# One layer of a gMLP and convolution decoder on eight cores: the mixer in one pass, the convolution on column tiles, normalisations beside the matmuls

## Chip, cores, metric

The kernel runs on all 8 cores of one Trainium2 chip, each on its own tokens with the same weights. The metric is the time of the slowest core in microseconds (us). Most executions agree within 0.3%. Some fall in a slower state, in which the cores of one die, sometimes of both, are granted a lower Tensor engine clock; those are kept out of every comparison here. PE is the Tensor engine, PEld its weight loads, DVE the Vector engine, ACT the Scalar engine, POOL GpSimd and SP the Sync engine.

## The reference, cut

```python
# D_MODEL = D_A = D_B = 2048, D_FF = 5632, CHUNK = 128, K_CONV = 31
x = x + 0.5 * swiglu_ffn(rms_norm(x, ffn1_norm), ffn1_w_gu, ffn1_w_down)
h = rms_norm(x, mix_norm)
ua, va, glu_a, glu_b, gate_a, gate_b = split(h @ w_in)          # 6 x 2048
v   = layer_norm(gelu(va))
y_a = chunk_spatial_gating(gelu(ua), v, w_s, b_s) @ w_pa
g   = glu_a * sigmoid(glu_b)
c   = silu(layer_norm(depthwise_conv31(concat(conv_prev, g)) + b_dw))
y_b = c @ w_pb
x   = x + (sigmoid(gate_a) * y_a + sigmoid(gate_b) * y_b) @ w_out
x = x + 0.5 * swiglu_ffn(rms_norm(x, ffn2_norm), ffn2_w_gu, ffn2_w_down)
return rms_norm(x, final_norm), ...                             # and v and g states
```

Each core holds 1024 prompt tokens, 64 sample tokens (16 sequences of 4) and 30 to 32 tokens of history, which the convolution needs from the half before.

## The kernel before

Activations lie with channels on the partitions and tokens in the columns. Weights are float32 in memory and are cast to bfloat16 by the DMA that loads them. x is transposed on PE at the start, y at the end. The mixer runs twice, over 608 and then 512 columns, with a barrier of all engines between its stages. A normalisation stands in the foreground (this cut and the next are shortened):

```python
def rms(gidx, segs, Hout):
    for (x0, n, l0) in segs:
        for k in range(KC):                      # sq: a ring of two buffers
            ea = act(sq, X[:, k, x0:x0 + n], AF.Square)
            mm(bk, ONES, sq, k == 0, k == KC - 1, deps=[ea])
        # Sqrt on ACT, reciprocal on DVE, then 16 scalings on DVE
...
mixer_pass(0, True)        # segs (0, 512) and 96 columns of history and samples
mixer_pass(512, False)
```

The convolution multiplies by 31 diagonal 128x128 matrices for each block of 128 channels:

```python
edg = tt(DG, IDF.to_broadcast([128, 31, 128]), wdw.to_broadcast([128, 31, 128]), ALU.mult)
for k in range(31):
    mm(bc[:, 0:512], DG[:, k, :], GPB[:, k:k + 512], k == 0, k == 30)
```

Of the kernel before, what the change touches and what calls it, by code (L numbers as in the profile page):

```python
# [5 lines left out]
F32 = mybir.dt.float32  # L6
# [7 lines left out]
NT = 1120  # L14
NPV = 9 * 16 + 31 * 16
PV_F1, PV_MIX, PV_F2, PV_FIN, PV_BDW, PV_LCG, PV_LCB, PV_LVG, PV_LVB = range(9)
PV_WDW = 9 * 16
EPS = 1e-6
ENGS = ["pe", "act", "dve", "pool", "sp"]
NSLOT = 4  # L20
SLOT_B = 8192

OFF_X = 0
OFF_PV = 71680
OFF_IDF = OFF_PV + 2560
OFF_ONES = OFF_IDF + 512
OFF_EPS = OFF_ONES + 256
OFF_GTAIL = OFF_EPS + 16
OFF_WST = OFF_GTAIL + 1920
OFF_MS = OFF_WST + 4096  # L30
OFF_SMALL = OFF_MS + 2048
PL0 = 83456
assert OFF_SMALL + 256 <= PL0
OFF_RSTD = PL0
OFF_SLOTS = OFF_RSTD + 4608
OFF_TMPX = OFF_SLOTS + NSLOT * SLOT_B
REG0 = OFF_TMPX + 12288
OFF_H = REG0
OFF_HID = REG0 + 35840
OFF_HM = REG0  # L40
OFF_V = REG0 + 19456
OFF_US = OFF_V + 20480
OFF_CN = OFF_US + 18432
ARENA_B = REG0 + 78848

class Plan:
    def __init__(self):
        self.q = {e: [] for e in ENGS}
        self.n = {e: 0 for e in ENGS}
        self.waited = {e: {} for e in ENGS}  # L50
        self.dcnt = {}
        self.needed = {e: set() for e in ENGS}

    def wait(self, eng, ev):
        if ev is None:
            return
        k, v = ev
        if self.waited[eng].get(k, 0) >= v:
            return
        self.waited[eng][k] = v  # L60
        if k in self.needed:
            self.needed[k].add(v)
        self.q[eng].append(("wait", k, v))

    def op(self, eng, fn, deps=()):
        for d in deps:
            self.wait(eng, d)
        self.n[eng] += 1
        self.q[eng].append(("op", fn, self.n[eng]))
        return (eng, self.n[eng])  # L70

    def dma(self, eng, out, in_, semkey, deps=()):
        for d in deps:
            self.wait(eng, d)
        c = self.dcnt.get(semkey, 0) + 16
        self.dcnt[semkey] = c
        self.q[eng].append(("dma", out, in_, semkey))
        return (semkey, c)

    def last(self, eng):  # L80
        return (eng, self.n[eng]) if self.n[eng] > 0 else None

class Ring:
    def __init__(self, items):
        self.items = items
        self.i = 0
        self.free = [[] for _ in items]

    def get(self):
        idx = self.i % len(self.items)  # L90
        self.i += 1
        return idx, self.items[idx], list(self.free[idx])

    def release(self, idx, events):
        self.free[idx] = [e for e in events if e is not None]

def build_program(stop_after=None):
# [7 lines left out]

    xin = din("xin", [NT, D])
    cache = din("cache", [16, 30, D])
    pv_d = din("pv", [128, NPV])
    identf_d = din("identf", [128, 128])
# [7 lines left out]
    w_gu1 = din("w_gu1", [44, 128, 4096])  # L117
    w_dn1 = din("w_dn1", [32, 128, 2816])
    w_v = din("w_v", [8, 128, 4096])
    w_u = din("w_u", [8, 128, 4096])  # L120
    w_glu = din("w_glu", [16, 128, 4096])
    w_gate = din("w_gate", [16, 128, 4096])
    w_pab = din("w_pab", [16, 128, 4096])
    w_out = din("w_out", [8, 128, 4096])
    w_gu2 = din("w_gu2", [44, 128, 4096])
    w_dn2 = din("w_dn2", [32, 128, 2816])

    y_o = dout("y", [1088, D])
    vlast_o = dout("vlast", [128, D])
    vsamp_o = dout("vsamp", [64, D])  # L130
    csp_o = dout("csp", [30, D])
    cssn_o = dout("cssn", [64, D])
    csso_o = dout("csso", [16, 26, D])

    P = Plan()

    with nc.sbuf_tensor("arena", [128, ARENA_B // 4], F32) as arena, \
            nc.psum_tensor("ps", [128, 8, 512], F32) as ps:

        def view(off, shape, dt=F32):  # L140
            esz = 4 if dt == F32 else 2
            n = int(np.prod(shape))
            a = arena[:, off // 4:(off + n * esz) // 4]
            if dt != F32:
                a = a.bitcast(dt)
            if len(shape) == 2:
                a = a.rearrange("p (a b) -> p a b", a=shape[0])
            elif len(shape) == 3:
                a = a.rearrange("p (a b c) -> p a b c", a=shape[0], b=shape[1])
            return a  # L150

        X = view(OFF_X, [KC, NT])
        PV = view(OFF_PV, [NPV])
        IDF = view(OFF_IDF, [128])
        ONES = view(OFF_ONES, [128], BF16)
        EPSV = view(OFF_EPS, [4])
        GTAIL = view(OFF_GTAIL, [KC, 30])
        WST = view(OFF_WST, [16, 128], BF16)
        MS = view(OFF_MS, [16, 64], BF16)
        SMALL = view(OFF_SMALL, [64])  # L160
        ST = SMALL[:, 0:24]
        MV = SMALL[:, 24:26]
        RS1 = SMALL[:, 28:29]
        RSTD = view(OFF_RSTD, [1152])
        slots = [view(OFF_SLOTS + i * SLOT_B, [4096], BF16) for i in range(NSLOT)]
        H = view(OFF_H, [KC, NT], BF16)
        HID = view(OFF_HID, [11, NT], BF16)
        HM = view(OFF_HM, [KC, 608], BF16)
        V = view(OFF_V, [5, D], BF16)
        MM_ = view(OFF_V, [KC, 576], BF16)  # L170
        US = view(OFF_US, [KC, 576], BF16)
        CN = view(OFF_CN, [KC, 576], BF16)

        banks = Ring([ps[:, b, :] for b in range(8)])
        wring = Ring(slots)

        def mm(out, lhsT, rhs, start, stop, deps=()):
            return P.op("pe", lambda e: e.matmul(out, lhsT, rhs, start=start, stop=stop), deps)  # L178

        def tr(out, in_, ident, deps=()):  # L180
            return P.op("pe", lambda e: e.transpose(out, in_, ident), deps)  # L181

        def act(out, in_, func, deps=(), **kw):
            return P.op("act", lambda e: e.activation(out=out, in_=in_, func=func, **kw), deps)  # L184

        def cp(eng, out, in_, deps=()):
            if eng == "act":
                return P.op("act", lambda e: e.copy(out=out, in_=in_), deps)  # L188
            return P.op(eng, lambda e: e.tensor_copy(out=out, in_=in_), deps)  # L189

        def tt(out, in0, in1, op, deps=(), eng="dve"):
            return P.op(eng, lambda e: e.tensor_tensor(out=out, in0=in0, in1=in1, op=op), deps)  # L192

        def ts(out, in0, s1, s2, op0, op1, deps=(), eng="dve"):
            return P.op(eng, lambda e: e.tensor_scalar(out=out, in0=in0, scalar1=s1, scalar2=s2,
                                                       op0=op0, op1=op1), deps)

        def stt(out, in0, scalar, in1, op0, op1, deps=(), eng="dve"):
            return P.op(eng, lambda e: e.scalar_tensor_tensor(out=out, in0=in0, scalar=scalar, in1=in1,  # L199
                                                              op0=op0, op1=op1), deps)  # L200

        def barrier():
            evs = [P.last(e) for e in ("pe", "act", "dve", "pool")]
            evs = [e for e in evs if e is not None]
            for ok_ in sorted(k for k in P.dcnt if k.startswith("o_")):
                evs.append((ok_, P.dcnt[ok_]))
            for e in ("pe", "act", "dve"):
                for ev in evs:
                    if ev[0] != e:
                        P.wait(e, ev)  # L210
            return evs

        w_hold = []

        def wload(parts, extra=()):
            idx, slot, free = wring.get()
            ev = None
            extra = list(extra) + list(w_hold)
            del w_hold[:]
            for i, (dst_fn, src) in enumerate(parts):  # L220
                ev = P.dma("pool", dst_fn(slot), src, "w%d" % idx, deps=(free + list(extra)) if i == 0 else ())
            return idx, slot, ev

        def wk(slot, n):
            return slot[:, 0:16 * n].rearrange("p (k n) -> p k n", n=n)

        def colblk(w, c0, n):
            return w[:, c0:c0 + n].rearrange("(k p) n -> p k n", p=128)

        MT = view(OFF_H, [128])  # L230
        MSK = view(OFF_H + 512, [64])
        WCOL = view(OFF_H + 1024, [16, 4])
        WSTT = view(OFF_H + 2048, [16, 128])
        c_ev = None
        for dst, src in ((PV, pv_d), (IDF, identf_d), (MT, maskt_d), (MSK[0:64], masks_d),
                         (WCOL[0:64], wcol_d), (WSTT, wst_d)):
            c_ev = P.dma("sp", dst, src, "c0")
        P.op("dve", lambda e: e.memset(ONES, 1.0))
# [10 lines left out]
        for t in range(9):  # L249
# [3 lines left out]
            if t == 6:  # L253
                w_hold.append(lev)
# [450 lines left out]
        if stop_after != "p0":  # L705
            ffn(PV_F1, w_gu1, w_dn1)
# [204 lines left out]
```

## Time and profile before

| | before |
|---|---|
| median of the runs before the prediction | 3789.4 us (4 runs) |
| profiled run, slowest core | 3786.8 us |
| PE busy, share of the span | 3507.9 us, 93% |
| mean granted clock | 0.957 |
| DMA moved | 328 MB |

A busy PE is not a PE at its peak: matmuls are pipelined, so their rate has to be read from pieces of the chain of waits and not from the mean of one instruction. The prediction below shows these pieces, the windows by stage and the waits.

### The profile page before, as it was taken

How to read it: one execution, taken by the hardware profiler on the slowest of the kernel's cores; microseconds unless marked ns; L12 is line 12 of the kernel's file. 1: busy time of each engine (PE TensorE's matmuls, PEld its weight loads, DVE VectorE, ACT ScalarE, POOL GpSimd, SP SyncE). 2: the span in 40 equal slices, each digit the busy share in tenths (PEclk: the TensorE clock that was granted, in tenths of full speed). 3: DMA queues.
4: the chain of work that ended last, by engine and by line, in shares of the span. 5: the costliest groups of instructions: out<-in, count | busy, mean ns of one | idle time of the engine just before them, and what ended most of it. 6: DMA issues, size and time to landing. Idle time of an engine off the chain costs nothing.

```text
span 3786.8 us, 53265 instructions; the slowest of 8 cores (3777.8 to 3786.8 us)
## 1 busy us (share of the span) xinstructions
PE 3507.9 (93%) x22280; PEld 2021.7 (53%) x22280; DVE 937.4 (25%) x1517; ACT 501.2 (13%) x970; POOL 170.1 (4%) x316
## 2 busy tenths in 40 slices
PE   5999999999976999879977998799899999999996
PEld 3666666666645555435545443344466666666663
DVE  5112121121132433331122433211412112112125
ACT  3000000000012111221112112200300000000003
POOL 0000000000000000000000000000000000000000
PEclk7999999999988999989988999899899999999997
DMA  8334334343335443247656643588333434334332
GB/s 194 67 58 83 64 65 78 58 83 67 58 82 102 91 96 82 53 82 136 132 119 126 119 79 57 101 152 146 69 64 65 78 57 83 67 58 83 64 54 95
DMA packets 50537, 328.44 MB, mean 87 GB/s; under 512 B 6208, under 2 KB 7968, under 8 KB 17248
## 3 DMA queue, kind: packets, MB, share of 16 engines
q0 software_dynamic: 43904, 293.36, 42.7%
q1 hardware_dynamic: 6400, 31.67, 2.7%
q8 instruction: 182, 2.98, 0.3%
q14 instruction: 51, 0.42, 0.0%
HBM read 603.16 MB, written 14.66 MB: 163 GB/s over the span
## 4 chain that ended last, share of the span: by engine, by line
PE 90%; DVE 4%; ACT 2%; DMA 2%; issue 1%; DVEq 0%; SPq 0%; ACTq 0%; POOLq 0%
PE ps L178 90%; DVE arena L199 2%; ACT arena L184 2%; DVE arena L192 1%; DMA arena<-xin 1%; PE ps L181 1%; DVE arena L382 0%; DMA y<-arena 0%; ACT L184 0%; DVE arena L286 0%; DVE arena L633 0%; DVE arena L727 0%; DMA arena<-cache 0%; DMA vsamp<-arena 0%; DMA vlast<-arena 0%
## 5 line engine op out<-in xcount | busy, mean ns | idle before, releaser
L178 PE MATMUL ps<-arena 128*128 128x374 bf16 (+5 forms) x21896 | 3459.2, 319 | 221.8 <-ACT arena L184 117.2
L178 PEld LDWEIGHTS ps<-arena 128*128 128x128 bf16 x21896 | 1973.8, 98 | 1703.3 <-issue 319.4
L192 DVE TENSOR_TENSOR arena<-arena,ps 128x374 bf16<-128x374 f32 (+6 forms) x424 | 221.3, 527 | 1709.0 <-PE ps L178 1175.1
L184 ACT ACTIVATE arena<-ps 128x374 f32<-128x374 f32 (+5 forms) x528 | 246.5, 467 | 2508.0 <-PE ps L178 2504.7
L199 DVE SCALAR_TENSOR_TENSOR arena<-ps,arena 128x374 f32<-128x374 f32 (+3 forms) x451 | 244.2, 547 | 528.8 <-PE ps L178 528.0
L192 DVE TENSOR_TENSOR arena<-arena 128x512 bf16<-128x512 f32 (+5 forms) x198 | 245.2, 1251 | 194.7 <-PE ps L181 161.2
L184 ACT ACTIVATE arena<-arena 128x512 bf16<-128x512 f32 (+9 forms) x277 | 159.8, 613 | 353.0 <-DVE arena L199 180.1
L199 DVE SCALAR_TENSOR_TENSOR arena<-arena 128x374 bf16<-128x374 f32 (+7 forms) x204 | 103.1, 578 | 2.6
L181 PE MATMUL ps<-arena 128*128 128x128 f32 (+4 forms) x384 | 58.5, 306 | 48.7 <-DMA arena<-xin 28.4
L787 POOL DMA_DIRECT2D arena<-w_gu x88 | 46.7, 531 | 1202.9 <-PE ps L178 1156.3
L181 PEld LDWEIGHTS ps<-arena 128*128 128x128 f32 (+4 forms) x384 | 49.4, 157 | 53.0 <-issue 51.0
L787 POOL DMA_DIRECT2D arena<-w_dn x64 | 33.8, 529 | 794.9 <-PE ps L178 794.9
L184 ACT ACTIVATE arena<-ps,arena 128x512 bf16<-128x512 f32 (+6 forms) x60 | 37.5, 624 | 213.2 <-PE ps L178 213.1
L382 DVE BATCH_NORM_STATS2 arena<-arena 128x6 f32<-128x512 bf16 (+1 forms) x36 | 22.2, 679 | 121.8 <-ACT arena L184 121.6
L192 DVE TENSOR_TENSOR arena<-ps,arena 128x512 f32<-128x512 f32 (+1 forms) x64 | 27.7, 454 | 97.3 <-PE ps L178 97.3
L184 ACT ACT_TABLE_LOAD x20 | 25.7, 1283 | 132.8 <-PE ps L178 99.6
L787 POOL DMA_DIRECT2D arena<-w_pab x32 | 16.9, 529 | 457.4 <-PE ps L178 457.4
L188 ACT COPY arena<-ps 128x512 f32<-128x512 f32 (+4 forms) x68 | 30.8, 464 | 47.6 <-PE ps L181 35.7
L286 DVE RECIPROCAL arena<-arena 128x374 f32<-128x374 f32 (+3 forms) x9 | 22.3, 2482 | 50.9 <-ACT arena L184 50.9
L189 DVE COPY arena<-ps 128x512 f32<-128x512 f32 (+2 forms) x36 | 23.7, 680 | 34.4 <-PE ps L181 24.4
L787 POOL DMA_DIRECT2D arena<-w_glu x32 | 17.3, 542 | 182.7 <-PE ps L178 182.7
L787 POOL DMA_DIRECT2D arena<-w_gate x32 | 16.9, 529 | 144.1 <-PE ps L178 138.4
(19 smaller groups left out, 83.0 us busy)
## 6 DMA issues: line engine op xcount, KB each, us to landing
arena<-w_gu POOLq DMA_DIRECT2D x88, 1024.0 KB, 8.0
arena<-w_dn POOLq DMA_DIRECT2D x64, 704.0 KB, 6.3
arena<-w_glu POOLq DMA_DIRECT2D x32, 1024.0 KB, 8.1
arena<-w_pab POOLq DMA_DIRECT2D x32, 1024.0 KB, 8.6
arena<-w_gate POOLq DMA_DIRECT2D x32, 1024.0 KB, 9.3
arena<-w_v POOLq DMA_DIRECT2D x16, 1024.0 KB, 8.8
arena<-w_u POOLq DMA_DIRECT2D x16, 1024.0 KB, 8.6
arena<-w_out POOLq DMA_DIRECT2D x16, 1024.0 KB, 9.0
```

Source lines behind the costliest of these rows:

```text
L178: return P.op("pe", lambda e: e.matmul(out, lhsT, rhs, start=start, stop=stop), deps)
L181: return P.op("pe", lambda e: e.transpose(out, in_, ident), deps)
L184: return P.op("act", lambda e: e.activation(out=out, in_=in_, func=func, **kw), deps)
L188: return P.op("act", lambda e: e.copy(out=out, in_=in_), deps)
L189: return P.op(eng, lambda e: e.tensor_copy(out=out, in_=in_), deps)
L192: return P.op(eng, lambda e: e.tensor_tensor(out=out, in0=in0, in1=in1, op=op), deps)
L199: return P.op(eng, lambda e: e.scalar_tensor_tensor(out=out, in0=in0, scalar=scalar, in1=in1, op0=op0, op1=op1), deps)
L286: er = P.op("dve", lambda e, l0=l0, n=n: e.reciprocal(out=RSTD[:, l0:l0 + n], in_=RSTD[:, l0:l0 + n]), deps=[ea])
L382: e0 = P.op("dve", lambda e, q=q, t=t, rows=rows, STp=STp: e.bn_stats(out=STp[0:rows, q * 6:(q + 1) * 6], in_=V[0:rows, t, q * 512:(q + 1) ...
L787: ins = e.dma_start(out=item[1], in_=item[2])
```

## The change

The intent was to take away PE columns and PE idle time together. The host hands over x and takes y channel by channel, so that the transposes go. The mixer runs once over all columns. The convolution keeps four shifted copies of its input on four groups of 32 partitions, so that one matmul covers four taps of 32 channels. Four such matmuls, with their outputs on four groups of 32 columns of the array (column tiles), cover four taps of a block of 128 channels, and eight such quads cover its 31 taps. The normalisations that follow an FFN or the output projection begin beside its last pass. Barriers are replaced by dependencies tracked by memory cell. To make room, x is spilled to memory during the mixer. The core of the diff, with comments added:

```diff
-NT = 1120
+NP_ = 1024
+NS = 64
+NH = 30
+NM = NP_ + NS
+NT = NM + NH
-NSLOT = 4
+NSLOT = 5
...
-            for k in range(31):
-                lc = mm(bc[:, 0:512], DG[:, k, :], GPB[:, k:k + 512], k == 0, k == 30, ...)
+            P.dma("sp", gs_d[c % 2], g, wk=[("gs", c % 2)])             # spill g
+            for s in range(4):                                          # read it back shifted by s
+                P.dma("sp", g4[32 * s:32 * s + 32, :, 0:GPN], src[:, :, s:s + GPN], ...)
...
+            for (c0, n) in ((0, 512), (512, 512), (1024, 64)):
+                bk = bank()
+                for q in range(8):
+                    for j in range(4):
+                        mm(bk[32 * j:32 * j + 32, 0:n], dg[:, q, j, :], rhs, q == 0, q == 7)
...
-        mixer_pass(0, True)
-        mixer_pass(512, False)
...
+        P1 = [[(0, 384), (384, 384)], [(768, NT - 768)]]    # last down pass of FFN1, in two
+        def after_m1(pi, o, m, seg):
+            add_square(X1, m, o == 0, *seg)
+            if pi == 1:
+                if o == 0:
+                    stats1(0)
+                    stats1(1)
+                bgpop(1 if o < 3 else 2)                     # scalings of the norm, one or two at a time
```

## The prediction

> **What bounds the kernel now.** I read the page's busy shares first, then the matmuls by shape, then one table of windows cut at the stage borders (found in the chain of waits in order of time), then the waits of the Tensor engine. The Tensor engine (PE) is busy 93% of 3786.8 us; no other engine passes 25%. By shape:
>
> ```profile
> L178 PE MATMUL ps<-arena 128*128 128x374 bf16 x8512 | 1404.8, 323 | 24.0 <-ACT arena L184 16.5 <-DVE arena L192 7.2
> L178 PE MATMUL ps<-arena 128*128 128x512 bf16 x5224 | 1182.1, 383 | 150.5 <-ACT arena L184 84.7 <-DMA vsamp<-arena 29.0 <-DMA vlast<-arena 24.8
> L178 PE MATMUL ps<-arena 128*128 128x64 bf16 x1824 | 71.3, 196 | 3.5 <-ACT arena L184 3.5
> ```
>
> The means (323 ns for 374 columns) are latencies of pipelined instructions; the rate is in the chain. A piece of 1584 matmuls is one FFN quarter (1056 gate/up, 528 down):
>
> ```profile
> 252.71 250.81 PE ps L178 x1584
> 504.41 250.81 PE ps L178 x1584
> 1585.49 1.22 PE ps L178 x8
> ```
>
> From 252.71 to 504.41 are 251.70 us for 1584 matmuls of 373.3 columns on average: 158.9 ns each, that is 373.3/2.4 = 155.6 ns plus 3.3 ns. So inside a stage nothing but columns counts. The windows show where that is not so (columns: busy us and count of PE, PEld, DVE, ACT, POOL, then clock, DMA share, GB/s):
>
> ```profile
> 0.00:95.00 95.00, 54.40 (x258) 31.85 (x259) 48.62 (x75) 37.35 (x73) 2.46 (x8) 0.78 0.86 193
> 95.00:1099.00 1004.00, 997.29 (x6281) 610.01 (x6279) 176.22 (x324) 68.63 (x140) 40.17 (x76) 1.00 0.38 70
> 1099.00:1128.00 29.00, 10.09 (x38) 4.36 (x38) 18.46 (x34) 9.44 (x25) 0.00 (x0) 0.50 0.23 73
> 1199.00:1306.00 107.00, 76.26 (x596) 42.26 (x596) 51.69 (x115) 28.29 (x45) 3.17 (x6) 0.86 0.37 75
> 1306.00:1583.00 277.00, 270.02 (x2096) 148.79 (x2096) 89.37 (x96) 42.90 (x97) 23.32 (x35) 0.98 0.45 89
> 1583.00:1631.00 48.00, 9.96 (x65) 4.15 (x66) 29.44 (x39) 27.48 (x37) 0.00 (x0) 0.64 0.00 1
> 2388.00:2675.00 287.00, 281.94 (x1286) 126.52 (x1286) 44.14 (x64) 23.21 (x40) 21.14 (x40) 0.99 0.84 144
> 3716.00:3786.80 70.80, 40.08 (x190) 24.19 (x189) 43.08 (x69) 32.98 (x67) 0.00 (x0) 0.67 0.34 127
> ```
>
> Long windows run at PE 97 to 99% and clock 0.98 to 1.00; the seams (start, normalisations, end) run nearly empty and at a clock down to 0.50. So the mean clock, 0.957, comes from idle seams and not from density. The waits name what stands in the seams:
>
> ```profile
> PE ps L178 <- ACT arena L184: 117.2, 94, 36.3
> PE ps L178 <- DVE arena L199: 31.4, 4, 16.5
> PE ps L178 <- DMA vsamp<-arena: 29.0, 1, 29.0
> PE ps L181 <- DMA arena<-xin: 28.4, 7, 15.2
> PE ps L178 <- DMA vlast<-arena: 24.8, 1, 24.8
> ```
>
> **What the Trainium skill says.** (1) "TensorE: Matmul & The Clock Gate", section "Back-to-back issue gap", gives N/2.4 + 2.5 ns for a warm matmul; the trace agrees within 1 ns (158.9 against 158.1), for weights loaded behind the stream. (2) The same page, "Seeing it yourself", says all-core dense matmul should be budgeted at 13/16 of the clock. The trace disagrees: 1.00 over a thousand microseconds on eight cores. I therefore do not expect a denser kernel to be throttled. (3) The same page, "Measured speedup vs the span model", has three column tiles of 32 outputs running 2.38 times as fast as one after another; "TensorEngine Tiling", "Restrictions", adds that column tiling gives up the fast weight load. No run here shows it; the kernel before has no such matmul. (4) "VectorE: DVE Perf Modes", "The perf-mode tier table", gives 693 ns for a 2048-element bf16 tensor_scalar in SBUF. No instruction before shows it (its f32 two-input pass of that width took 2.29 us).
>
> **The change part by part.** It is a rewrite: dependencies are tracked by memory cells rather than barriers, the mixer runs once over all columns instead of in two token halves, x and y come transposed from the host, and the convolution is remapped.
>
> Dense parts before, from the chain: FFNs 2 x 6336 x 158.9 ns = 2014 us; v projection 132; u and spatial gating 137; GLU and convolution 487 (16 periods of 16.73 in the first half, 13.71 in the second); merge and output projection 599. Sum 3370; the other 417 us are seams.
>
> Dense parts after, at N/2.4 + 3.3 ns:
> - FFN1: 1118 columns instead of 1120: 2112 x (1118/2.4 + 10) = 1005 us. FFN2 drops the history columns and runs 1088: 1936 x 463.4 ns + 176 x 465 ns = 979. Together 1984, saving 30.
> - v projection: 576 matmuls of 512 columns instead of 1152 of 256, at 217 ns (63 convolution matmuls of the second half take 13.7 us): 125, saving 7.
> - GLU: 512 x (1118/2.4 + 10) = 244, saving 2. u: 256 x 463.4 = 119, plus 144 small spatial matmuls at about 60 = 9; 127, saving 10. Merge and output: 1280 x 463.4 = 593, saving 6; the sliver matmuls of 64 and 96 columns, which cost about 50 ns (63 of them in 16.73 - 13.6 = 3.1 us), are gone there.
> - Convolution: before, 31 diagonal 128x128 matmuls per channel block, 512 columns twice and 64 once: 16 x (31 x 2 x 217.8 + 31 x 50 ns) = 241 us. After, the history is stored four times with shifts on four partition groups, so one matmul handles 4 taps of 32 channels and writes 32 outputs; 8 tap groups x 4 channel groups, the four being column tiles that may run together. Full overlap would be 8 x 1088/2.4 x 16 = 58 us. I allow 240 ns for a quad of 512 columns (256 quads, 61 us) and 110 for one of 64 (128, 14 us), an estimate between full overlap and the skill's 79% efficiency (2.38 of 3): 75, saving 166.
>
> Sum after 3148, saving 222.
>
> Seams. Start, about 90 us before the first steady FFN matmul: the 256 f32 transposes of x and their evictions go, what remains is the load: 9.2 MB at an estimated 200 to 300 GB/s (the hardware queue before moved 31.67 MB in 2.7% of the span of 16 engines, 310 GB/s, with larger packets), three weight tiles squeezed in, then one sum of squares. All three segments' sums stand before the first gate matmul in PE order, so I put it at 50 us. End, 71 us: y is stored untransposed and two thirds of the final norm run during the last down passes. But the last pass, 128 columns, takes PE only 10 us while Vector scales a 512 segment in it (3.35 reciprocal + 16 x 0.74) and adds 32 small ops of about 0.25: 23 us. So 12 us of backlog, then the last segment's chain (table load 1.28, reciprocal 0.9, 16 x 0.34, a store of 3): 25 us in all. Inside: the two entry norms, two v layernorms, two conv layernorms and the FFN2 norm, some 250 us, become background work. I leave 45: 5 at FFN1 to v, 6 where the v layernorm (about 23 us of Vector) outlasts the 20 us that eight banks let PE run ahead, 12 where the conv sums, six f32 matmuls and three root/reciprocal chains precede the u stage, 9 at its end and at FFN2's entry, and 13 for cold clock and Vector's load in the u stage (2.25 us of 2.7 per segment). Seams after: 120.
>
> 3148 + 120 + 2 (launch, as before) = 3270; I add 10 for the unseen and say 3280 us.
>
> **Rivals.** A: the column tiles do not overlap. Then 1024 x 217 + 512 x 40 ns = 242 us instead of 75, and the kernel takes about 3445. For it: no such matmul in the trace; against: the skill's measurement. B: transfers become the bound in the GLU and convolution stage. Each channel block now moves 1.05 MB of weights (FFN window: 70 GB/s at share 0.38, so 5.7 us of all engines), 0.4 MB of spill and 1.6 MB of shifted reads in pieces of 1 to 2 KB (7 to 9 us): some 16 us in a 20 us period. Tight; if the small pieces are twice as dear the stage grows by 50 to 80 us, to 3340. Two blocks of run-ahead speak against latency trouble. C: full density brings throttling, 13/16 on all matmuls: over 3700. The clock of 1.00 in both FFNs speaks against. D: Vector or the new GpSimd multiplies (48 of 364 columns, none in the trace before) become the bound of the u stage: 20 to 40 us. E: the seams close wholly: 3235. That the weight loads of the mixer halve (share 0.84 in the second merge) gains nothing: that window is already at PE 98%.
>
> **Range and chances.** A at about 8%, B at 15%, D at 15% (parts of them overlap), the start and end uncertain by 20 us each way: 3225 to 3370 eight times in ten. Everything except C is more than 2% faster: faster 0.97, same 0.02, slower 0.01.
>
> **What would show it.** Right: FFN pieces still at about 158.9 ns, mean clock 0.98 or more, GLU and convolution at about 20 us per channel block, PE over 96% busy, first FFN matmul near 50 us, tail near 25. Wrong: a convolution block of 15 us instead of 5 (A); PE waiting for the shifted copies with the DMA share near 1 (B); FFN clock under 0.95 (C); PE waiting for Vector in the u stage (D).

## The result

The changed kernel takes 3273.14 us (median of 11 runs, 3270.82 to 3887.81, slow ones included) against 3792.83 (16 runs). The ratio is 0.8631, with a 95% interval of 0.8621 to 0.864. A ratio here is the mean time of one kernel's fast runs over that of the other's in the same rounds, so it is not quite the ratio of the medians. The prediction was 3280, 7 us high.

The first profile of it fell in the slow state, so it was profiled again among the experiments, unedited, under the name e0_after:

> The changed kernel itself, unedited, beside the edited ones on the same chip, and for a profile in the fast state. Expected 3273 us, as in its first runs, mean clock 0.99 on both dies; it is the mark that the other runs are compared with.

On that chip die 0 was granted a little less clock in every run, and the median was 3291.63 (ratio 0.8685, 0.8659 to 0.8711). Die 1 was undisturbed. For this reason I read core 6, on die 1, and compare kernels below also by the median core of an undisturbed die: 3265.4 us for the unedited kernel (the first result's fast runs have 3262.8 to 3267.2 on both dies). The cores of that profile:

```profile
die 0 (median of its cores): 3283.5 us, clock 0.985
die 1 (median of its cores): 3265.6 us, clock 0.991
```

The same windows as in the prediction, cut at the new stage borders (busy us and count of PE, PEld, DVE, ACT, POOL, then clock, DMA share, GB/s). They are the start, FFN1, the entry of v, v, GLU and convolution, the way to u, u, merge and output, FFN2, and the end:

```profile
0.00:50.00 50.00, 17.60 (x43) 4.46 (x43) 22.07 (x37) 21.25 (x47) 2.53 (x9) 1.00 0.89 232
50.00:1056.50 1006.50, 1005.64 (x6346) 614.44 (x6345) 216.52 (x397) 92.38 (x186) 41.25 (x78) 1.00 0.42 70
1056.50:1068.10 11.60, 0.05 (x1) 0.03 (x1) 9.02 (x19) 1.98 (x5) 0.54 (x1) 0.61 1.01 163
1068.10:1196.20 128.10, 128.09 (x579) 57.47 (x580) 36.73 (x57) 25.28 (x39) 3.17 (x6) 0.98 0.81 185
1196.20:1508.00 311.80, 302.09 (x2976) 178.47 (x2975) 111.33 (x202) 72.25 (x144) 18.19 (x33) 0.99 0.83 172
1508.00:1545.00 37.00, 18.36 (x155) 9.77 (x156) 16.23 (x24) 8.17 (x13) 0.00 (x0) 0.80 0.27 65
1545.00:1668.00 123.00, 122.82 (x871) 79.87 (x869) 106.98 (x216) 82.67 (x142) 49.54 (x55) 1.00 0.33 61
1668.00:2261.00 593.00, 592.38 (x3849) 375.44 (x3850) 140.87 (x269) 73.06 (x148) 23.93 (x46) 1.00 0.50 91
2261.00:3229.40 968.40, 964.68 (x6165) 602.59 (x6163) 207.22 (x375) 88.00 (x170) 39.67 (x75) 1.00 0.44 77
3229.40:3267.10 37.70, 15.30 (x180) 13.43 (x177) 27.90 (x68) 6.66 (x19) 1.59 (x3) 0.69 0.76 198
```

In the kernel before, nine of the seventeen windows of the full table, of which the prediction shows eight, had PE busy for less than three quarters of the time; here four of ten have, and two of them are 12 and 37 us long. What PE still waits for on this core (us in all, times, longest). L299, and L300 in some edits, is the helper that issues all matmuls; L303 is the one for ACT, and L309, L313, L318 and L322 are those for DVE:

```profile
PE ps L299 <- ACT arena L303: 32.7, 12, 10.2
PE ps L299 <- DMA arena<-gspill: 15.7, 1, 15.7
PE ps L299 <- DVE arena L309: 12.8, 8, 3.4
PE ps L299 <- DMA arena<-w_v: 11.6, 1, 11.6
PE ps L299 <- DMA arena<-w_dn: 10.4, 3, 4.8
```

The waits for ACT are those at the start (they follow the arrival of x). The transfers of `gspill` (the scratch tensor through which the shifted copies go), `w_v` (weights of v) and `w_dn` (weights of an FFN's down product) are waits that did not exist before. The column tiles, by shape (busy us, mean ns of one):

```profile
L299 PE MATMUL ps<-arena 128*32 128x512 bf16 x1024 | 60.1, 389 | 16.2 <-DMA arena<-gspill 15.7 <-issue 0.5
L299 PE MATMUL ps<-arena 128*32 128x64 bf16 x512 | 6.9, 193 | 0.0
```

The 1024 wide ones are busy for 60.1 us, which is 59 ns each: four run together, since one alone would take 216 ns. Busy time is a poor measure for comparing orders: it counts the end of each stretch, which the next matmuls overlap, and where two shapes alternate it counts that time under both. So I compare convolutions by starts instead, from the first convolution matmul of a channel block to the next matmul of another kind. That is 3.88 us a block here in the steady part of the stage, 62 us for 16 blocks; 64 wide matmuls take 3.46 us of it, 54 ns each. In the kernel before it was 234 us by the same measure (62 starts of 216 ns and 31 of 40 ns a block).

### The profile page after: what moved, and what is told of

It reads as the page before. It is cut to its first block, busy times and chain, and to the rows that moved or that the text cites. A ratio compares the mean times of both kernels' runs of the same rounds, so it can differ in the third digit from the quotient of the medians.

```text
span 3470.6 us, 50849 instructions; the slowest of 8 cores (3262.2 to 3470.6 us)
## 1 busy us (share of the span) xinstructions
PE 3369.9 (97%) x21154; PEld 2010.4 (58%) x21154; DVE 895.4 (26%) x1660; ACT 473.0 (14%) x910; POOL 179.8 (5%) x304
## 4 chain that ended last, share of the span: by engine, by line
PE 93%; DMA 4%; SPq 1%; DVE 1%; issue 1%; ACT 0%; DVEq 0%; POOL 0%; ACTq 0%; POOLq 0%
PE ps L299 93%; DMA gspill<-arena 1%; SPq L943 1%; DMA arena<-gspill 1%; DMA arena<-xin 1%; DMA arena<-w_v 0%; DMA arena<-w_dn 0%; DVE arena L309 0%; DVE arena L318 0%; DVE arena L313 0%; DVE arena L322 0%; ACT arena L303 0%; ACT L303 0%; DVEq L935 0%; SPq L937 0%
## 5 line engine op out<-in xcount | busy, mean ns | idle before, releaser
L299 PE MATMUL ps<-arena 128*128 128x364 bf16 (+11 forms) x21154 | 3369.9, 334 | 91.7 <-ACT arena L303 33.3
L299 PEld LDWEIGHTS ps<-arena 128*128 128x128 bf16 (+2 forms) x21154 | 2010.4, 101 | 1450.9 <-issue 132.7
L309 DVE TENSOR_TENSOR arena<-arena,ps 128x374 bf16<-128x374 f32 (+7 forms) x456 | 223.6, 499 | 1843.7 <-PE ps L299 1843.7
L303 ACT ACTIVATE arena<-ps 128x364 f32<-128x364 f32 (+6 forms) x492 | 238.3, 485 | 2543.9 <-PE ps L299 2533.0
L318 DVE SCALAR_TENSOR_TENSOR arena<-ps,arena 128x364 f32<-128x364 f32 (+8 forms) x467 | 243.4, 527 | 451.4 <-PE ps L299 451.0
L309 DVE TENSOR_TENSOR arena<-arena 128x384 f32<-128x384 f32 (+14 forms) x361 | 228.4, 641 | 71.6 <-ACT arena L303 62.3
L303 ACT ACTIVATE arena<-arena 128x384 f32<-128x384 f32 (+9 forms) x293 | 163.1, 569 | 310.6 <-DVE arena L318 153.7
L318 DVE SCALAR_TENSOR_TENSOR arena<-arena 128x384 bf16<-128x384 f32 (+11 forms) x245 | 133.6, 591 | 3.4 <-ACT arena L303 1.9
L303 ACT ACTIVATE arena<-ps,arena 128x512 bf16<-128x512 f32 (+6 forms) x108 | 53.9, 565 | 88.7 <-PE ps L299 88.7
L309 POOL TENSOR_TENSOR arena<-arena 128x364 f32<-128x364 f32 (+1 forms) x48 | 45.7, 952 | 122.7 <-DVE arena L309 122.7
L322 DVE RECIPROCAL arena<-arena 128x384 f32<-128x384 f32 (+11 forms) x17 | 37.0, 2178 | 47.0 <-ACT arena L303 47.0
L309 DVE TENSOR_TENSOR arena<-ps,arena 128x384 f32<-128x384 f32 (+1 forms) x48 | 25.6, 533 | 54.1 <-PE ps L299 39.2
L313 DVE TENSOR_SCALAR arena<-arena 128x2048 bf16<-128x2048 bf16 (+4 forms) x12 | 9.4, 838 | 0.0
## 6 DMA issues: line engine op xcount, KB each, us to landing
arena<-w_gu POOLq DMA_DIRECT2D x88, 1024.0 KB, 10.1
```

The lines of the kernel that those rows point to most:

```text
L299: return P.op("pe", lambda e: e.matmul(out, lhsT, rhs, start=start, stop=stop), [lhsT, rhs], [out])
L303: return P.op("act", lambda e: e.activation(out=out, in_=in_, func=func, **kw), rd, [out])
L309: return P.op(eng, lambda e: e.tensor_tensor(out=out, in0=in0, in1=in1, op=op), [in0, in1], [out])
L313: return P.op("dve", lambda e: e.tensor_scalar(out=out, in0=in0, scalar1=s1, scalar2=s2, op0=op0, op1=op1), rd, [out])
L318: return P.op("dve", lambda e: e.scalar_tensor_tensor(out=out, in0=in0, scalar=s, in1=in1, op0=op0, op1=op1), rd, [out])
L322: return P.op("dve", lambda e: e.reciprocal(out=out, in_=in_), [in_], [out])
```

## The experiments

All kernels below are edits of the changed kernel. Unless it is said otherwise they give correct results. "Die median" is the median core of an undisturbed die in the fast runs, or in runs that are slow by the other die alone; the unedited kernel has 3265.4.

### Issuing the column tiles group by group

```diff
-                for q in range(8):
-                    for j in range(4):
+                for j in range(4):
+                    for q in range(8):
```

> The 32 convolution matmuls of a channel block are issued one column group after the other (8 in a row on the same 32 output columns) instead of one from each group in turn; same matmuls, same result. Theory (the gain of the convolution is the running together of four column tiles): each matmul of 512 columns then takes 213 to 220 ns instead of 59, the convolution 16 x (64 x 217 + 32 x 30 to 40 ns) = 235 to 245 us instead of 68, less up to 18 us of waits for the shifted copies that it now covers: 3273 + 150 to 175 = 3423 to 3448 us. Rival (the gain comes from the mapping, fewer tap groups, and the order is indifferent, or from another place): 3273 us, within 10.

Measured: 3347.29 us, ratio 0.8821; die median 3325.8, so 60 us more. Neither theory held. The convolution matmuls of this run:

```profile
L299 PE MATMUL ps<-arena 128*32 128x512 bf16 x1024 | 131.5, 386 | 6.9 <-DMA arena<-gspill 6.9
L299 PE MATMUL ps<-arena 128*32 128x64 bf16 x512 | 17.7, 194 | 0.0
```

That is 128 ns each, as if two ran together; by starts it is 110 ns, and the block takes 8.23 us, 132 us for all 16. The trace's start times of one block tell how. These are the distances in ns between successive starts of its wide matmuls, here and in the unedited kernel:

```
group by group: 227 216 216 216   5 210  17 199  17 199  17 216   5 210  17 199 ...
one of each:      3   3   4 216   4   3   5 204   4   3   5 204 ...
```

Group by group, four matmuls start alone and from then on they start in pairs, until the matmuls of 64 columns follow. This fits a machine that starts a matmul of the next column group while the one before still has about four to go. The records do not say which group a start belongs to, so I made a second order to test it.

### The group loop outside all chunks

```diff
-            for (c0, n) in ((0, 512), (512, 512), (1024, 64)):
-                bk = bank()
-                for q in range(8):
-                    for j in range(4):
+            cb = [bank() for _ in range(3)]
+            for j in range(4):
+                for (c0, n), bk in zip(((0, 512), (512, 512), (1024, 64)), cb):
+                    for q in range(8):
```

> After the first ordering run the starts in its trace came in pairs 17 and 199 ns apart: a column group that has work was started up to about four matmuls ahead of the group before it. Here the group loop is outermost over the three column chunks, 24 matmuls in a row on one group. New theory (groups run together only within a short look-ahead of about four matmuls): only the small ends overlap, the matmuls of 512 columns take about 205 to 216 ns each, the convolution 215 to 235 us, and with the waits for shifted copies covered the kernel takes 3273 + 135 to 165 = 3408 to 3438 us. Rival (two groups always run together whatever the order, since some other resource feeds two): as in the first ordering run, 55 to 65 us above the unedited kernel.

Measured: 3426 us in both fast runs, ratio 0.9027; die medians 3416 to 3420, about 153 us more. The new theory's range held, the rival's did not.

```profile
L299 PE MATMUL ps<-arena 128*32 128x512 bf16 x1024 | 230.5, 380 | 0.0
L299 PE MATMUL ps<-arena 128*32 128x64 bf16 x512 | 26.0, 193 | 0.0
```

Now the starts of the wide matmuls are 216 ns apart. With 24 in a row on one group only the ends of the groups overlap, and a block takes 14.57 us, which is 233 us for the convolution, as much as the 234 of the kernel before (the two busy times above add up to 256.5 us, but the shapes alternate here and their overlap is counted twice). So the new mapping alone, with its shifted copies and its fewer tap groups, gains nothing: all of the gain comes from four groups running together, and for that they must be issued in turn, or within about four of each other. The wait of 15.7 us for `gspill` is gone in this run, because the slower convolution hides it; that is most of why 171 us more of convolution cost only 153.

### The normalisations back in the foreground

```diff
-        P1 = [[(0, 384), (384, 384)], [(768, NT - 768)]]
+        P1 = [[(0, 384), (384, 384), (768, NT - 768)]]
         ffn("gu1", "dn1", H1, HID1, X1, S1, P1, ...)
+        for si in range(3):
+            stats1(si)
+        bgpop(100)
```

The output projection and the last pass of FFN2 are edited in the same way, and the reloads of weights for the later passes go.

> The last down pass of each FFN and the output projection run over all columns in one pass, and the three normalisations after them follow it in the foreground, instead of two thirds of each running beside the last pass. Theory (seams closed by work beside the last pass carry much of the gain): about 12 us more at FFN1 to v, where the 11 us wait for the v weights is then covered, 12 at the FFN2 entry, 14 at the end: 3295 to 3325 us. Rival (what closed the seams is the removal of the barriers and of the transposes alone; the split passes give little): within 10 us of 3273.

Measured: only one run of four was fast, 3308.6 us, so there is no ratio. The die medians of the undisturbed die are 3297.7 to 3300.6, 33 us more. The direction and the size are the theory's. One part of it was wrong: the wait for the first v weights was not covered, it grew to 17.3 us. In the chain of this run (start us, us, what) the FFN2 entry stands in the foreground again, as the lines show, and so does the end, where the same reciprocals and scalings fill the chain from 3263 to 3295 us:

```profile
2267.91 2.56 DVE arena L322
2270.57 2.27 DVE arena L318 x5
2273.22 5.90 DVE arena L318 x11
2279.12 2.48 DVE arena L322
2282.05 2.28 DVE arena L318 x5
2284.70 3.27 DVE arena L318 x6
2290.76 968.11 PE ps L299 x6289
```

The 33 us are three of the seams. The other seams of the kernel before, and its second pass over the mixer, are not in this run.

### FFN2's gate and up over 1118 columns

```diff
+            gsegs = S1 if gu == "gu1" else [(0, 374), (359, 374), (718, 370)]
...
-                    for seg in segs:
+                    for seg in gsegs:
                         gate_up(gu, j, jj, H, HID, seg)
```

> The gate and up matmuls of FFN2 run over overlapping segments of 374, 374 and 370 columns, 1118 as before the change, instead of 1088; the doubled columns are computed twice with the same values. Theory (inside a stage nothing but columns counts): 1408 x 30 / 2.4 ns = 17.6 us more, 3291 us, within 3. Rival (fixed cost per matmul or another engine sets the pace, the shorter segments save nothing): within 4 us of 3273.

Measured: 3308.91 us, ratio 0.8722 beside 0.8685 for the unedited kernel on the same chip; die medians 3284.2 to 3285.8, 19.5 us more against 17.6 expected. In these stages columns are what is paid for.

### Weight traffic of the merge doubled

```diff
                     P.dma("pool", slots[s][:, 0:w], wd[nm][i], ...)
+                    if nm in ('pab', 'gate'):
+                        P.dma("pool", dup_d[('pab', 'gate').index(nm) * 16 + i], wd[nm][i])
```

> Every weight tile of the merge (32 tiles) is also loaded and cast a second time into a scratch tensor in memory, so that the transfers of that stage double, about as much weight traffic as the two-half mixer had. Theory (halving the loads gained nothing, the stage was and is bound by matmul columns): within 5 us of 3273, DMA share of the merge windows from 0.44 to 0.8 or more. Rival (the halved loads were part of the gain): 15 us or more slower.

Measured: 3308.7 us in the fast runs, ratio 0.8718; die medians 3299 to 3302, 35 us more. This is the rival's figure, but the window shows that the edit overshot, since the DMA engines had no room left:

```profile
1678.00:2160.00 482.00, 457.03 (x2930) 285.98 (x2928) 72.54 (x136) 43.54 (x92) 30.25 (x57) 0.99 1.00 134
```

A share of 1.00 was never reached in the merge of the kernel before (0.68 in the first, 0.84 in the second), so this run does not decide. With only one of the two weights of a channel block doubled:

> The doubling of all 32 merge tiles filled the DMA engines (share 1.00) and so overshot. Here only 16 of them are loaded a second time. At about 8 us of all engines for a doubled tile the share of the merge windows should go from 0.46 to 0.70 to 0.75, near what the second merge of the kernel before had (0.84). Theory (below saturation the weight traffic costs nothing, so halving it gained nothing): within 5 us of the unedited kernel, 3268 to 3278 us on a chip with both dies undisturbed. Rival (traffic slows the weights that PE waits for well before saturation): 10 us or more slower.

Measured: 3273.9 us in both fast runs; die medians 3264 to 3268, no difference. The share was 0.71 and PE was never idle in that window:

```profile
1678.00:2160.00 482.00, 482.00 (x3131) 304.71 (x3129) 80.30 (x151) 47.55 (x100) 24.27 (x46) 1.00 0.71 111
```

Up to a share of 0.71 weight traffic beside the merge costs nothing, and in the kernel before PE was busy for 98% of the window with a share of 0.84; at 1.00 it costs 35 us. So loading the merge's weights once instead of twice gained no time by itself, as far as the kernel before goes. Whether the changed kernel could carry the full double load below saturation is not shown, and the next run shows that it could not in the GLU stage.

### Weight traffic of the GLU stage doubled

The same edit for `glu`.

> The same doubling for the 16 GLU tiles, in the stage whose DMA share is 0.85. Theory (that stage is close below its DMA bound): 16 x 5.7 us of engine time more than fit, the stage of 290 us grows by 20 to 60 us: 3293 to 3333 us, with PE waiting for shifted copies or GLU weights. Rival (the share counts time in which packets wait, and there is much room): within 8 us of 3273.

Measured: 3376.57 and 3398.36 us in the fast runs, ratio 0.8925; die medians mostly 3368 to 3374, about 105 us more, above the theory's range. What PE waits for:

```profile
PE ps L300 <- DMA arena<-gspill: 103.3, 9, 30.5
PE ps L300 <- ACT arena L304: 31.9, 12, 8.8
```

So the GLU and convolution stage, at a share of 0.83, stands just inside its DMA bound, and the prediction's rival B was near. My 5.7 us for a doubled tile was too small. From the unedited merge window (share 0.46) and the second merge run one costs (0.71 - 0.46) x 482 / 16 = 7.5 us of all engines, which is 120 us for 16. About 53 us of that fitted into the free 0.17 of 312 us. The other 67 us are less than the 105 us measured: in this run the share is 0.91 over the 424 us from 1196 to 1620, so the engines also stood idle for 38 us while PE waited, and it is not bandwidth alone that PE waits for.

### The last three down tiles kept resident

```diff
+        TAILW = [view(OFF_B + i * 5632, [2816], BF16) for i in range(3)]
...
+                if pi == 1 and len(passes) == 3:
+                    for i in range(3):
+                        P.dma("pool", TAILW[i], wd["dn2"][29 + i])
```

> The three down tiles that are loaded again during the 128-column last pass are loaded once into the memory of the FFN2 input, which is dead by then. Theory (the 9.6 to 10.4 us of PE waits for these reloads lengthen the end): 5 to 10 us less, 3263 to 3268 us, the waits for w_dn gone. Rival (Vector, busy 23.6 of the last 30 us, takes their place): 0 to 3 us less.

Measured: 3275.37 us, ratio 0.8628; die medians 3265 to 3268, no difference. The rival was right: the waits for `w_dn` are gone, and another took their place.

```profile
PE ps L299 <- ACT arena L303: 32.1, 11, 8.8
PE ps L299 <- DVE arena L309: 28.6, 11, 9.2
PE ps L299 <- DMA arena<-gspill: 14.0, 1, 14.0
```

After 3120 us PE's waits were 10.4 us for `w_dn` and 4.7 for DVE; now they are 13.3 us for DVE alone, since in the last pass of 128 columns DVE scales the segment before. (Of the rise from 12.8 to 28.6 us in the lines above, 9.2 us is at the entry of v, on which the next section has more.) The chain at the end now alternates between DVE and ACT:

```profile
3242.24 0.95 DVE arena L318 x2
3243.27 0.32 ACT arena L303
3243.64 0.15 issue
3243.81 0.15 issue
3243.96 0.95 DVE arena L318 x2
```

### The spill of x a quarter of v later

```diff
-                if pr == 0:
+                if pr == 1:
                     for m in (2 * t, 2 * t + 1):
                         P.dma("sp", xs_d[m], X1[:, m, 0:NM], wk=[("xs", m)])
...
-            if pr == 0:
+            if pr == 1:
                 P.dma("sp", LNG, lnvg_d.to_broadcast([128, D]))
```

> The spill of the residual stream, 16 transfers at the start of the v projection, is moved one quarter of that stage later, and the constant loads behind it too. Theory (the first v weights take 16 us to land instead of 8 because the spill runs beside them, and the 11 us wait at the entry of v comes from that): the wait falls to 3 to 6 us, the kernel to 3265 to 3268 us. Rival (the weights are issued late, when their slot comes free, and would be waited for anyway; or the later spill delays the v layernorm): 0 to 2 us less, or slower.

Measured: 3276.24 us (3273.6 and 3273.9 for the two quickest runs), ratio 0.8638; die medians about 3266, no difference. The rival was right. PE's wait went from 11.6 to 10.1 us on core 6. In the chain the transfer that it waits for, from issue to landing, hardly moved, without and with the edit:

```profile
1051.09 16.67 DMA arena<-w_v
```

```profile
1049.89 15.12 DMA arena<-w_v
```

The spill is not what these weights compete with. They are issued when the last down tiles free their slots. The unedited trace shows what they meet there. From 1040 to 1068 us the engines' time went to these queues (packets, MB, share of 16 engines); q0 carries the weight loads and q1 the spill:

```profile
q0 software_dynamic: 653, 3.96, 89.8%
q1 hardware_dynamic: 29, 0.13, 1.2%
```

Three tiles of v are issued within 1.6 us of each other, and they compete among themselves; the spill has hardly begun. Nor would quicker weights have gained much. In the run of the next section, as in the one before, the weights of v came first on core 6, and PE still waited 9.2 us at the same place, now for DVE, which was finishing the last additions of FFN1 and the scalings of the norm:

```profile
PE ps L299 <- DVE arena L309: 22.3, 9, 9.2
```

So two waits of 9 to 12 us stand beside each other at the entry of v, and removing one alone is worth little (11.6 less 9.2 us on core 6).

### The u tiles held until the last spill has landed

```diff
+            if c == KC - 1:
+                W.hold[("u", 0)] = [sp_]      # sp_: the spill of the last block
+                W.add(rest)                   # u and everything after it
+                W.pump()
```

> The u weight tiles are held back until the last GLU block's spill has landed. Theory (the 14 to 16 us wait for the last shifted copies comes from weight loads running beside the spill): the wait falls to 8 to 11 us, the kernel to 3266 to 3270 us. Rival (the wait is the latency of two transfers one after the other with nothing left to hide it): wait unchanged, within 2 us of 3273, or a new wait for the u weights.

Measured: 3284.85 us, ratio 0.8658; die medians 3277 to 3280, 12 us more. Neither expectation held: the wait grew.

```profile
PE ps L299 <- ACT arena L303: 31.6, 12, 8.5
PE ps L299 <- DMA arena<-gspill: 25.0, 1, 25.0
```

The wait for the last shifted copies grew from 15.7 to 25.0 us. The held tiles are released together just when the copies are read back, and in the chain that read took 24.35 us instead of 7.39, while the spill before it took 2.77 instead of 11.79. So neighbours in the queue do set this wait, but I had moved them to the worse of its two transfers. Holding the tiles until the read has landed was not tried.

### Late spill, held u tiles, and x before the first weights

```diff
-        W.hold[("gu1", 0)] = xev[0][2:3]
-        W.hold[("gu1", 1)] = xev[1][2:3]
-        W.hold[("gu1", 2)] = xev[2][2:3]
+        W.hold[("gu1", 0)] = xev[1][2:3]
+        W.hold[("gu1", 1)] = xev[2][2:3]
+        W.hold[("gu1", 2)] = xev[2][3:4]
```

> The late spill and the held u tiles together, and the first weight tiles held until more of x has landed. Theory (weight tiles that load beside x delay the start by their share of the engines): the first FFN matmul at 42 to 46 us instead of 51, and with the other two 3255 to 3264 us. Rival (the start is bound by the rate of the 1.5 KB pieces of x, not by the weights): start unchanged or a wait for the second tile, 3266 to 3273 us.

Measured: all six runs were slow by one die (3437.9 to 3926.9), so there is no time to quote. The undisturbed die has 3268 to 3274, 6 us more than unedited. The start did what the theory said; unedited and edited chain:

```profile
51.02 978.95 PE ps L299 x6175
```

```profile
44.27 979.38 PE ps L299 x6175
```

Those 6.7 us are won and the 12 of the held u tiles are lost. The start edit alone should give about 3266 us, an estimate (3273 less 6.7); it was not run alone. None of my kernels beat the changed one in a whole run.

## Why the prediction was right, point by point

The total was right, and most terms of the sum were. On core 6 of e0_after, borders from the chain and from the first and last matmul of each shape:

| step | predicted us | measured us |
|---|---|---|
| start | 50 | 51 |
| FFN1 | 1005 | 1005 (51.0 to 1056.5) |
| v | 125 | 128 |
| GLU | 244 | 244 (16 x 15.2) |
| convolution | 75 | 62 (16 x 3.88, by starts) |
| u | 127 | 126 (1534 to 1668 less waits of 7.5) |
| merge and output | 593 | 592 |
| FFN2 without its last pass | 969 | 968 |
| last pass and end | 35 | 38 |
| seams inside | 45 | 52 (what is left of 3267) |

That the total came within 7 us is in part luck: the convolution was 13 us too high, and v, the seams and the end together were 14 us too low. The terms of the sum add up to 3268; the prediction added 2 for the launch and 10 for the unseen.

**What bounds it.** Columns over the clock was the right law: the FFN stages keep the rate that was read from the chain (158.5 ns for each of the 6175 matmuls of the first piece of FFN1), and the run with 30 more columns cost 19.5 us against 17.6. The page that the prediction cites for this rate gives the formula for an isolated matmul and says that it over-counts in a stream of 512 columns; here streams of 512 columns keep it, with starts 216 ns apart.

**The convolution.** The term was 13 us too high, and rival A was refuted by the two orders: 54 ns a matmul with the groups in turn, 216 with none together. The wide quads came out at 216 ns where I had allowed 240, and the eight small ones of a block at about 50 where I had allowed 110. The 75 did not lie between full overlap (58) and the page's efficiency (58 / 0.79 = 73), as the prediction has it, but just above both.

**Throttling, rival C.** Right for the fast state: the clock is 0.99, and 1.00 in both FFN windows. In the slow state the fraction that the page gives, 13/16, does appear. In the slow profile of the changed kernel (3472.15 us) core 3 ran at 0.81 from 200 to 1000 us and at 1.00 from 1800 us on, and a run at 3887.81 us has means of 0.818 to 0.825 on die 0. One of these windows:

```profile
400.00:600.00 200.00, 200.00 (x1049) 113.80 (x1047) 24.65 (x46) 12.56 (x26) 6.33 (x12) 0.81 0.34 50
```

I had written that the trace disagrees; it disagrees for fast runs only. Five of the 11 runs of the result were slow and 4 of the 16 of the kernel before; whether the denser kernel falls into that state more often is not shown.

**Transfers, rival B.** The stage was as tight as I had reckoned (a share of 0.83, against 16 us of 20), and doubling a third of its traffic made it the bound. But the doubled tile cost more than my 5.7 us.

**Vector and GpSimd in u, rival D.** It did not come true: PE was busy for 122.82 of the 123 us from 1545 to 1668, though DVE was busy for 106.98.

**Seams.** The sum of the inside, 45 against 52, was nearly right for a list that was right in part. The way from the convolution's statistics to u came as expected: PE waited 3.4 and 7.4 us for DVE between 1521 and 1545 us, where I had 12. The v layernorm cost 1.3 us instead of 6, and Vector's load in u nothing. At the entry of v I had 5; it was 11.6, for the v weights with Vector's 9.2 beside them. The last shifted copies (15.7) were not on the list. The weights I had not looked for. For the copies I had argued that two blocks of run-ahead hide the latency, which is true for fourteen blocks and false for the last, after which nothing is left to hide it. At the end I had the Vector backlog right and missed the reload of the three down tiles; as the resident tiles showed, these two stand beside each other, so the sum held (28 us against 25; the terms written in the prediction add up to 23).

**Density against seams.** By the prediction's split, 222 us come from fewer columns (166 of them in the convolution) and 297 from seams. Measured on core 6, the seams and the two ends are now 51 + 52 + 28 (the end without 10 us of matmuls) = 131 instead of 417 us, 286 less. The remainder of the difference of the spans, 3786.8 - 3267.1 - 286 = 234 us, is dense work. The runs undid the overlap of groups (153) and three of the seams (33) one by one. That the other seams closed through the removed barriers, the removed transposes and the single pass is read from the two traces; no run undid those alone, and how they share these seams is not shown.

## What to carry to other kernels

Read the matmul rate and the seams apart: columns times clock gives the dense part to about a percent, and the seams have to be listed one by one, including the last round of each pipeline, where run-ahead no longer hides anything. Column tiles pay only if neighbouring matmuls in program order go to different column groups; check the distances of the starts. When a transfer is waited for, find out what shares the engines with it at that moment and what engine comes next, before moving anything: of four attempts on such waits here one helped, and that only in the chain. Where two waits stand beside each other, removing one uncovers the other.

## What the Trainium skill lacked or had wrong

- "TensorE: Matmul & The Clock Gate", "Measured speedup vs the span model": three column tiles are given as 2.38 times as fast as one after another, and four in a stream are not given. In a stream of 128x32 tiles with 512 columns four ran 4.0 times as fast (54 against 216 ns from start to start), with starts within a quad mostly 3 to 5 ns apart and a period of about 216 ns.
- The same page, "The mechanism", says that matmuls start in strict program order. The group-by-group order gave pairs of starts (17 and 199 ns apart); I found no reading of them but that a matmul of the next column group starts about four matmuls early, but which group a start belongs to is not in the records. No page that I found says how far apart in program order column tiles may be and still run together.
- The same page, "Wait — 56ns, not 53.3ns?": start to start is said never to drop below about 25 ns. Matmuls of 64 columns in a row on one group kept to that (28 to 34 ns), but with the groups in turn the 32 starts of a block took 0.24 us, 8 ns each.
- The same page, "Seeing it yourself": all-core dense matmuls are to be budgeted at 13/16. Fast runs of both kernels had 0.99 to 1.00 through both FFNs on eight cores; 13/16 (0.81) stood in stretches of slow runs.
- "VectorE: DVE Perf Modes", "The perf-mode tier table": 693 ns for a bf16 tensor_scalar of 2048 elements; here eight of them lasted 800 ns each, with starts 723 ns apart.
- No page that I found tells how long a load takes beside others: a weight tile of 1 MB landed in 8 us (median, FFN of the kernel before), and in 20.1 us (median of the eight tiles of v in the changed kernel, three of them issued within 1.6 us, in a stage with a DMA share of 0.81).
